# Where the gain and bias of the first feed-forward part's norm are applied to the residual rows

## The chip, the cores and the metric

The kernel runs on one core of a Trainium2 chip. The metric is the device time of one run in microseconds (us). The core has a matmul engine (TensorE, PE in the rows), a vector engine (VectorE, DVE), a scalar engine (ScalarE, ACT), a general engine (GpSimd, POOL) and a queue engine (SyncE, SP) that issues most transfers. Each engine works through its own list of instructions, and semaphores between the lists carry the dependences.

## The reference

The reference is a two-layer encoder trunk in float32 on 512 tokens of width 1024. Layer 0 mixes tokens by latent attention, layer 1 by a Hyena operator; a gated feed-forward part of width 2816 follows each. Behind every part stands the same residual norm:

```python
x <- layer_norm(DEEPNORM_ALPHA * x + f(x), g, b)      # (x - mean) * rsqrt(var + eps) * g + b

def hyena_mixer(x, ...):
    u = dwconv_centred(x @ w_in, w_short)             # 3 x 1024 features, a 3-tap convolution along the tokens
    v, g1, g2 = jnp.split(u, 3, axis=-1)
    z = v
    for o, gate in enumerate((g1, g2)):
        z_f = jnp.fft.rfft(z, n=2 * length, axis=1)
        y = jnp.fft.irfft(z_f * k_f, n=2 * length, axis=1)[:, :length]
        z = gate * (y + d_bias[o] * z)
    return z @ w_o

def conv_ffn(x, w_up, w_conv, w_down):
    a, g = jnp.split(dwconv_centred(x @ w_up, w_conv), 2, axis=-1)
    return (silu(g) * a) @ w_down
```

The norm's gain g and bias b therefore go two ways: into the next part's input, and into the residual row that the next norm adds.

## The kernel before

The four parts run in turn: attention, feed-forward part 0, Hyena, feed-forward part 1. Every projection is a float32 product in three passes of matmuls with split operands (lines 281 to 283: `xh,whi`, `xl,whi`, `xh,wlo`). The high halves come from ScalarE (line 274 for activations, 341 for weights), the low ones from VectorE (line 276, and 344 or 380 for weights). The tokens lie in four tiles t of 128.

**The tail of a part** (`tail`) projects back to the model width in two halves of 512 columns (names `dn`). `residual` adds the stored row, 1.414 times it, on VectorE (line 671) and takes statistics (line 674); `norm` makes mean and scale (lines 695, 696, 441, 443, 445, 449) and the normalised row (line 714); `put_x` transposes it on TensorE (line 287, name `xTps`) and applies gain and bias in the transposed form on ScalarE (line 541, name `xg`), since there they lie along the partitions. The same normalised row is also the residual of the next part: `save` stores it to DRAM with GpSimd's DMA (line 735, name `xsave`), and the next tail's `loads` fetches it again (line 629, name `xres`).

**Where the stored row gets its gain and bias** depends on the argument `late`. Without it, the tail loads the two vectors as rows over all partitions (`lngb`, line 629), and `save` multiplies and adds them on GpSimd, two steps for each half of 512 columns (line 733): 16 products for the four tiles. With `late`, the row is stored bare; the next tail then loads the two vectors ahead of its rows, and `apply` puts them on with VectorE (line 654), again 16 products, before `residual` may use a row. Attention's tail and the Hyena tail are `late`, the first feed-forward tail is not. The last tail, whose output leaves the chip, has no `save`.

**The Hyena part** projects 24 features (name `u`, each 8 x 3 matmuls) and puts a short convolution on each (line 1208 on ScalarE, 1210 and 1212 on VectorE). Features of the first two kinds are then transposed (line 287, name `utps`). Eight filter steps `long_conv` follow, two orders of four channel chunks: a forward transform on TensorE (line 1596, name `dft`), a chain of products on VectorE (line 1573, names `zt`, `zf`, `kf`; 20 of 512 elements a row and 4 of 1024), and an inverse transform on TensorE (line 1655 for order 0, 1673 for order 1, name `inv`) with one more product (`u<-inv`). A forward transform has two pairs of matmul groups; all but the first two products of the chain need the second pair. The results of order 1 are split and are the left side of the tail's `dn` matmuls, so the tail's matmuls begin while the last filter steps run. The output weights come in pieces, and SP loads them, the first weights of feed-forward part 1 and the tail's rows in one order.

**What sets the order.** The program is written as tasks that name, before each instruction, its engine and a rough cost. A list scheduler (class `Order`) resumes whichever task could start first by those costs, also with a limited count of blocks, accumulators and convolution slots, and each engine's queue gets the instructions in that order. Nothing else orders them: an edit to one task can alter the order of all engines from there on.

Of the kernel before, what the change touches and what calls it, by code (L numbers as in the profile page):

```python
# [21 lines left out]
P = 128  # L22
# [22 lines left out]
# The program is written as tasks (generators) that name, before each  # L45
# instruction, its engine and rough cost. A small list scheduler resumes them in
# the order in which a core would get to them; each engine's queue gets that order.
# [38 lines left out]
class Pending:  # L86
    """An event that waits for n parts."""
# [12 lines left out]
class Order:  # L100
# [25 lines left out]
    def step(self, task, value):  # L126
        """Resume a task and keep it where its next request is looked for."""
# [16 lines left out]
    def run(self):  # L144
        while True:
# [41 lines left out]
            if r[1] == "PE":  # L187
                # its clock is halved until it has been busy for a while
                if start - self.free.get("PE", -1e9) > COLD:
                    self.cold = COLD  # L190
                if self.cold > 0.0:
                    more = min(cost, self.cold / 2)
                    self.cold -= 2 * more
                    cost += more
# [39 lines left out]
class Trunk:  # L234
# [35 lines left out]
    def split(self, hi, lo, src, n, t, psum=False):  # L270
        """hi, lo: float32r parts of src, exact to the last bits."""
# [17 lines left out]
    def weights(self, src, shape, own=True, low=None, cut=False):  # L289
        """A task that loads a piece of a weight, 4 KB a partition, and splits it; its event.  # L290
        own: in the room for weights, else in two blocks. low: where its low part lies in DRAM, if it does.
        cut: in two transfers."""
# [59 lines left out]
    def low_part(self, src, shape, prio):  # L352
        """A task that puts the low part of a piece of a weight into DRAM ahead of its use; its event."""
# [38 lines left out]
    def columns(self, prio):  # L392
        """The vectors that lie along partitions, one column for each 128 values; their event."""
# [12 lines left out]
    def reduce_angle(self, r, ang, wide, t):  # L406
        """r = ang less the nearest multiple of 2 pi, within [-pi, pi]."""
# [27 lines left out]
    def rsqrt(self, y, m, t):  # L435
        """y = (-2 m) ** -0.5 for a few columns, with one Newton step."""
# [15 lines left out]
    def fm(self, ps, w, n, x, after, halves=False):  # L452
        """ps [P features, S] = sum over k of w(k)^T x(k), float32 in three passes.
        x(k): (hi, lo, event of the first half of the tokens, event of the second)."""
# [22 lines left out]
    def setup(self):  # L477
# [6 lines left out]
        # the array's clock is full only after a few us of work  # L484
# [8 lines left out]
    class X:  # L493
        """Feature-major x in float32r parts: two tiles of 128 features a block."""
# [23 lines left out]
    def put_x(self, x, t, src, times, gain=None):  # L518
        """Token tile t of x from token-major src [P, D]; times: when each half is there.
        gain: event of the columns, and where a gain and a bias to apply on the way lie in them."""  # L520
# [30 lines left out]
    def load_x(self):  # L551
        """The transposed x, laid out as [4, P, 2, S]."""
# [29 lines left out]
    def tail(self, base, lhs, w, nk, g, b, last, free_lhs, late, low=(), beats=()):  # L582
        """x <- LayerNorm(ALPHA x + lhs^T w), token-major; lhs(k): (hi, lo, event).
        late: x is kept without its gain and bias, for the next part to apply. Returns the new x."""
# [31 lines left out]
        def loads():  # L616
# [3 lines left out]
            # the table of the square root ahead of the norm  # L620
# [27 lines left out]
        def apply(t, tm, pg):  # L648
            # the gain and the bias of the norm before
# [12 lines left out]
        def residual(t, half, pss, tms):  # L662
            """pss: the accumulators of a half's columns, tms: when they are there."""
# [15 lines left out]
        def tail_cuts(t, half):  # L679
            # the columns of a half; the last ones in two pieces  # L680
# [1161 lines left out]
```

## Time and profile before

| | us |
| --- | --- |
| median of 3 runs | 1267.77 |
| lowest, highest | 1266.93, 1268.64 |
| span of the profiled execution, from its first instruction to its last | 1262.5 |
| TensorE, VectorE, ScalarE, GpSimd busy in it | 1238.5, 943.5, 568.1, 81.6 |

The profile is of one execution. Its own time is not listed apart from the span; the median of the runs is 5.3 us above the span, and that is taken as what lies around it. Times in the rows count from the start of the span. The first feed-forward part's last `dn` matmul starts at 634.41 us, the first projection of the Hyena part at 642.64, the last inverse transform at 858.29, and the first `up` matmul of feed-forward part 1 at 891.31. A matmul's duration in a timeline includes its way through the array and overlaps the next one; what it costs TensorE is the distance to the next start. The same holds for VectorE, where the next operation starts a little before the last one's end. Idle time in brackets is that of the engine before the row, with the instruction that ended it.

### The profile page before, as it was taken

The page shows a single profiled execution, that of the slowest core. Times are in us where ns is not written, and L with a number is a line of the kernel's source. Part 1 is how long each engine was busy: PE and PEld are TensorE (multiplying, and loading weights), DVE is VectorE, ACT ScalarE, POOL GpSimd, SP SyncE. Part 2 cuts the span into 40 slices and gives each one's busy share as a digit, 9 for nine tenths or more (in the row PEclk, how much of TensorE's full clock was granted, in tenths as well). Part 3 has the DMA queues.
Part 4 walks back from the last instruction along what each step waited for, and adds up shares of the span by engine and source line. Part 5 has one row for each costly group of instructions (what it writes and reads, how often), then busy time and mean ns, then how long its engine had stood idle before and what let it go on. Part 6 is the DMA issues. An engine that isn't in the chain of part 4 may idle for free.

```text
span 1262.5 us, 16644 instructions
## 1 busy us (share of the span) xinstructions
PE 1238.5 (98%) x6246; PEld 1051.7 (83%) x6246; DVE 943.5 (75%) x1614; ACT 568.1 (45%) x1086; POOL 81.6 (6%) x140
## 2 busy tenths in 40 slices
PE   8999999999999999999979999999999999999997
PEld 6788888988888888888868888887988888888886
DVE  7898987799997678657677999996566665553626
ACT  5566655644444456534553333232744444433220
POOL 0101000000000001100260000000000000000000
PEclk9999999999999999999989999999999999999999
DMA  5201125543344378999955655456433322323621
GB/s 207 60 28 47 57 70 214 184 136 120 120 143 136 97 261 290 299 350 303 317 194 169 200 170 167 141 190 222 145 100 96 90 98 100 100 89 113 233 67 67
DMA packets 67020, 195.47 MB, mean 155 GB/s; under 512 B 6873, under 2 KB 10713, under 8 KB 66940
## 3 DMA queue, kind: packets, MB, share of 16 engines
q1 hardware_dynamic: 53692, 146.17, 35.4%
q0 software_dynamic: 13248, 48.24, 11.0%
q8 instruction: 49, 0.80, 0.3%
q14 instruction: 31, 0.25, 0.1%
HBM read 160.83 MB, written 33.55 MB: 154 GB/s over the span
## 4 chain that ended last, share of the span: by engine, by line
PE 90%; DVE 4%; DMA 3%; ACT 2%; SPq 0%; issue 0%; DVEq 0%; ACTq 0%
PE up L282 12%; PE up L281 12%; PE up L283 12%; PE dn L281 7%; PE dn L283 7%; PE dn L282 7%; PE u L282 3%; PE u L283 3%; PE u L281 3%; PE dft L1596 2%; PE pTps L287 1%; PE inv L1673 1%; DMA wraw<-in_ffn_w_down_dram 1%; PE inv L1655 1%; ACT xg L541 1%; DVE xl L276 1%
## 5 line engine op out<-in xcount | busy, mean ns | idle before, releaser
L281 PE MATMUL up<-xh,whi 128*128 128x512 f32 (+1 forms) x768 | 286.1, 372 | 0.0
L282 PE MATMUL up<-xl,whi 128*128 128x512 f32 (+1 forms) x768 | 285.5, 372 | 0.0
L283 PE MATMUL up<-xh,wlo 128*128 128x512 f32 (+1 forms) x768 | 285.2, 371 | 0.0
L341 ACT CAST whi<-wraw 128x512 fp32r<-128x512 f32 (+1 forms) x376 | 216.3, 615 | 121.7 <-PE dn L283 94.0
L344 DVE TENSOR_TENSOR wlo<-wraw,whi 128x512 fp32r<-128x512 f32 (+1 forms) x312 | 207.3, 678 | 80.4 <-ACT whi L341 80.1
L283 PEld LDWEIGHTS up<-xh,wlo 128*128 128x128 f32 x768 | 144.6, 188 | 25.1
L281 PEld LDWEIGHTS up<-xh,whi 128*128 128x128 f32 x768 | 144.7, 188 | 24.5
L282 PEld LDWEIGHTS up<-xl,whi 128*128 128x128 f32 x768 | 144.7, 188 | 24.3
L1210 DVE SCALAR_TENSOR_TENSOR cv<-up,cols,cv 128x511 f32<-128x511 f32 x88 | 65.6, 748 | 112.7 <-ACT cv L1208 112.7
L281 PE MATMUL dn<-whi,gated 128*128 128x512 f32 (+1 forms) x374 | 141.4, 378 | 0.1
L282 PE MATMUL dn<-wlo,gated 128*128 128x512 f32 (+1 forms) x374 | 140.9, 377 | 0.0
L283 PE MATMUL dn<-whi,gated 128*128 128x512 f32 (+1 forms) x374 | 140.9, 377 | 0.0
L1208 ACT ACTIVATE cv<-up,cols 128x512 f32<-128x512 f32 x88 | 60.4, 689 | 166.7 <-PE up L283 166.5
L281 PE MATMUL u<-xh,whi 128*128 128x512 f32 (+1 forms) x224 | 87.1, 389 | 0.0
L282 PE MATMUL u<-xl,whi 128*128 128x512 f32 (+1 forms) x224 | 81.5, 364 | 1.6 <-DVE xl L276 1.6
L281 PEld LDWEIGHTS dn<-whi,gated 128*128 128x128 f32 x374 | 70.4, 188 | 13.3 <-DVE xres L671 0.5
L283 PE MATMUL u<-xh,wlo 128*128 128x512 f32 (+1 forms) x224 | 81.3, 363 | 0.0
L283 PEld LDWEIGHTS dn<-whi,gated 128*128 128x128 f32 x374 | 70.4, 188 | 13.0
L282 PEld LDWEIGHTS dn<-wlo,gated 128*128 128x128 f32 x374 | 70.4, 188 | 12.7
L1212 DVE SCALAR_TENSOR_TENSOR cv<-up,cols,cv 128x511 f32<-128x511 f32 x88 | 65.2, 743 | 0.0
L1573 DVE TENSOR_TENSOR zf<-zt 128x512 f32<-128x512 f32 x80 | 51.5, 682 | 0.0
L541 ACT ACTIVATE xg<-xTps,cols 128x128 f32<-128x128 f32 x96 | 38.3, 466 | 27.2 <-PE xTps L287 27.2
(244 smaller groups left out, 2149.7 us busy)
## 6 DMA issues: line engine op xcount, KB each, us to landing
wraw<-in_ffn_up_dram SPq DMA_DIRECT2D x91, 512.0 KB, 3.6
wraw<-in_hy_in_dram SPq DMA_DIRECT2D x46, 512.0 KB, 6.8
wraw<-in_ffn_w_down_dram SPq DMA_DIRECT2D x44, 512.0 KB, 4.5
low<-wlo POOLq DMA_DIRECT2D x32, 512.0 KB, 7.2
wlo<-low POOLq DMA_DIRECT2D x32, 512.0 KB, 3.7
kf<-kfs POOLq DMA_DIRECT2D x16, 512.0 KB, 3.1
kf<-kf SPq DMA_DIRECT2D x16, 512.0 KB, 7.0
wraw<-in_hy_w_o_dram SPq DMA_DIRECT2D x15, 512.0 KB, 6.5
```

Of the source, the lines that this page charges most:

```text
L276: nc.vector.tensor_tensor(lo, src, hi.bitcast(F32), op=ALU.subtract)
L281: mm(ps, lh, rh, start=first, stop=False)
L282: mm(ps, lh, rl, start=False, stop=False)
L283: mm(ps, ll, rh, start=False, stop=last)
L341: nc.scalar.copy(hi[:, s], raw[:, s])
L344: nc.vector.tensor_tensor(lo[:, s], raw[:, s], hi[:, s].bitcast(F32), op=ALU.subtract)
L541: nc.scalar.activation(v[:, j, :], ps[:, j, :], AF.Identity, scale=gb[:, at + d:at + d + 1], bias=gb[:, at + ND + d:at + ND + d + 1])
L1208: nc.scalar.activation(dst, ps, AF.Copy, scale=taps(1))
L1210: nc.vector.scalar_tensor_tensor(dst[:, 1:], ps[:, :S - 1], taps(0), dst[:, 1:], op0=ALU.mult, op1=ALU.add)
L1212: nc.vector.scalar_tensor_tensor(dst[:, :S - 1], ps[:, 1:], taps(2), dst[:, :S - 1], op0=ALU.mult, op1=ALU.add)
L1573: tt = lambda d, a, b, f: nc.vector.tensor_tensor(d, a, b, op=f)
L1596: nc.tensor.matmul(q[:, w], tab[:, r, w], z[:, r], start=True, stop=True)
```

## The change

The first feed-forward tail becomes `late`, as attention's tail and the Hyena tail are. Its row loads of gain and bias and its 16 GpSimd products go, and its four stores hold bare normalised rows. The Hyena tail now loads gain and bias (two more transfers of 512 KB, ahead of its four rows, in two more blocks) and applies them with 16 VectorE products of 128 x 512 (line 654) ahead of line 671. The rest of the diff drops comments. Its core, in `ffn`:

```diff
@@ -1275,10 +1275,10 @@
         return self.tail(base + 2.0, lambda k: (gated[k] and gated[k][:, 0, :], gated[k] and gated[k][:, 1, :], gev[k]),
-                         a["ffn_w_down"][i], NF, a["ln2_g"][i], a["ln2_b"][i], last, free_lhs, False,
+                         a["ffn_w_down"][i], NF, a["ln2_g"][i], a["ln2_b"][i], last, free_lhs, not last,
                          beats=self.beats[2 * NF:] if i == 0 else [])
```

Since the tasks' steps and the blocks they hold differ, the scheduler writes the queues anew from the end of feed-forward part 0 to the end of the Hyena tail; from feed-forward part 1 on the order is the same. Three places show it.

**VectorE in the middle of the Hyena part.** A feature is projected (`u_6908`, `u_6956`), goes through the short convolution (`u_7143`, `u_7215`) and is transposed by TensorE (`utps_7289` before, `utps_7344` now). Before, the convolution's two steps stand here, the second of them 33 instructions on (counted with both) from the first product of the forward transform `dft_7100` (`zt_7006<-dft_7100`):

```order
L1573 TENSOR_TENSOR zt_7171<-dft_7182,e2_7186 128x512
L1573 TENSOR_TENSOR zt_7006<-zf_7004,kf_7002 128x1024
L1573 TENSOR_TENSOR zt_7171<-dft_7182,e2_7186 128x512
L1573 TENSOR_TENSOR kf_7002<-zf_7004,kf_7002 128x1024
L1210 SCALAR_TENSOR_TENSOR u_7143<-u_6908,cols_101,u_7143 128x511
L1573 TENSOR_TENSOR zf_7004<-kf_7002 128x512
L1212 SCALAR_TENSOR_TENSOR u_7143<-u_6908,cols_101,u_7143 128x511
L1573 TENSOR_TENSOR zf_7004<-zt_7006 128x512
L1573 TENSOR_TENSOR zt_7172<-dft_7278,e2_7282 128x512
```

In the changed queue, the second step of the counterpart stands 45 instructions on (counted with both) from the first product of `dft_7162` (`zt_7024<-dft_7162`), and another feature's steps (`u2_6963`) stand ahead of it:

```order
L1573 TENSOR_TENSOR zt_7111<-dft_7200,e2_7207 128x512
L1573 TENSOR_TENSOR zf_7021<-zt_7023,zt_7024 128x512
L1210 SCALAR_TENSOR_TENSOR u2_6963<-u_7002,cols_101,u2_6963 128x511
L1573 TENSOR_TENSOR zf_7021<-zt_7023,zt_7024 128x512
L1212 SCALAR_TENSOR_TENSOR u2_6963<-u_7002,cols_101,u2_6963 128x511
L1573 TENSOR_TENSOR zf_7022<-zt_7023,zt_7024 128x512
L1210 SCALAR_TENSOR_TENSOR u_7215<-u_6956,cols_101,u_7215 128x511
L1573 TENSOR_TENSOR zf_7022<-zt_7023,zt_7024 128x2x256
L1573 TENSOR_TENSOR zt_7112<-dft_7324,e2_7331 128x512
L1212 SCALAR_TENSOR_TENSOR u_7215<-u_6956,cols_101,u_7215 128x511
L1573 TENSOR_TENSOR zt_7112<-dft_7324,e2_7331 128x2x256
```

The convolution moved behind the whole chains of two filter steps. In the trace before, TensorE ends `dft_7100` at 728.76 and starts `utps_7289` at 753.91; now, between `dft_7162` and `utps_7344` lie 78 projection matmuls and two transforms.

**VectorE at the last filter step** (order 1, last chunk). Before, its products are mixed with the end of the step ahead (`u_7572`, its `xl`) and with short convolutions (`u_7694`), and TensorE has matmuls of several kinds between the last `dft` and the first of the last two `inv` groups:

```order
L1573 TENSOR_TENSOR zt<-zf,kf 128x1024
L1573 TENSOR_TENSOR u_7572<-inv,u_7572 128x4x128
L1573 TENSOR_TENSOR kf<-zf,kf 128x1024
L276 TENSOR_TENSOR xl<-u_7572,xh 128x512
L1573 TENSOR_TENSOR zf<-kf 128x512
L1212 SCALAR_TENSOR_TENSOR u_7694<-u,cols,u_7694 128x511
L1573 TENSOR_TENSOR zf<-zt 128x512
L1573 TENSOR_TENSOR u_7572<-inv,u_7572 128x4x128
L1573 TENSOR_TENSOR zt<-zf 128x512
L1210 SCALAR_TENSOR_TENSOR u_7694<-u,cols,u_7694 128x511
L276 TENSOR_TENSOR xl<-u_7572,xh 128x512
L1573 TENSOR_TENSOR zt<-zf 128x512
```

In the changed queue, the step's products stand by themselves, from its first to the end:

```order
L1212 SCALAR_TENSOR_TENSOR u_7662<-u,cols,u_7662 128x511
L1573 TENSOR_TENSOR zt<-dft,e_7977 128x512 x2
L1573 TENSOR_TENSOR zt<-dft,e_8006 128x512
L1573 TENSOR_TENSOR zt<-dft,e_8006 128x2x256
L1573 TENSOR_TENSOR zf<-zt 128x2x256 x3
L1573 TENSOR_TENSOR zf<-zt 128x512
L1573 TENSOR_TENSOR zt<-zf,kf 128x1024
L1573 TENSOR_TENSOR kf<-zf,kf 128x1024
L1573 TENSOR_TENSOR zf<-kf 128x512
L1573 TENSOR_TENSOR zf<-zt 128x512
L1573 TENSOR_TENSOR zt<-zf 128x512 x2
L1573 TENSOR_TENSOR zt<-zf,kf 128x1024
```

What was mixed in moved ahead of the chain, and on TensorE 18 `dn` matmuls now stand between the last `dft` and both last `inv` groups.

**VectorE in the Hyena tail**, from the last inverse products (`u<-inv`) to the first residual of token tile 0. Before:

```order
L1573 TENSOR_TENSOR u_7694<-inv,u_7694 128x4x128
L276 TENSOR_TENSOR xl<-u_7694,xh 128x512
L1573 TENSOR_TENSOR u_7694<-inv,u_7694 128x4x128
L276 TENSOR_TENSOR xl<-u_7694,xh 128x512
L344 TENSOR_TENSOR wlo<-wraw,whi 128x512 x2
L671 SCALAR_TENSOR_TENSOR xres<-xres,dn_7828 128x512
L344 TENSOR_TENSOR wlo<-wraw,whi 128x512 x2
L674 BN_STATS st<-xres 128x6
```

And in the changed queue:

```order
L1573 TENSOR_TENSOR u_7662<-inv,u_7662 128x4x128
L276 TENSOR_TENSOR xl<-u_7662,xh 128x512
L1573 TENSOR_TENSOR u_7662<-inv,u_7662 128x4x128
L276 TENSOR_TENSOR xl<-u_7662,xh 128x512
L654 TENSOR_TENSOR xres<-xres,lngb 128x512 x11
L344 TENSOR_TENSOR wlo<-wraw,whi 128x512 x2
L654 TENSOR_TENSOR xres<-xres,lngb 128x512 x4
L671 SCALAR_TENSOR_TENSOR xres<-xres,dn_7781 128x512
L654 TENSOR_TENSOR xres<-xres,lngb 128x512
L674 BN_STATS st<-xres 128x6
```

Fifteen of the 16 added products stand ahead of the first residual, eleven of them ahead of the low part of a weight piece (line 344). On SP the two row loads stand between the second weight load for feed-forward part 1 and the four `xres` loads.

## Rows read from the trace of the kernel before

**Rows 1.** The page: the busy line of the engines, the shares of the chain that ended last by engine, and of the costliest groups the gain and bias columns that ScalarE applies behind the transposes (busy us, mean ns of one, idle before).

```profile
PE 1238.5 (98%) x6246; PEld 1051.7 (83%) x6246; DVE 943.5 (75%) x1614; ACT 568.1 (45%) x1086; POOL 81.6 (6%) x140
...
PE 90%; DVE 4%; DMA 3%; ACT 2%; SPq 0%; issue 0%; DVEq 0%; ACTq 0%
...
L541 ACT ACTIVATE xg<-xTps,cols 128x128 f32<-128x128 f32 x96 | 38.3, 466 | 27.2 <-PE xTps L287 27.2
```

**Rows 2.** Busy time in stretches of 25 us: stretch, its length, busy us (and instructions) of PE, PEld, DVE, ACT and POOL, granted TensorE clock, DMA share, GB/s. The first stretch holds the end of the first feed-forward part and the start of the Hyena part, the second lies in the middle of the Hyena part, the third at its end.

```profile
625.00:650.00 25.00, 17.90 (x102) 15.75 (x101) 21.80 (x33) 15.37 (x43) 16.76 (x16) 0.86 0.58 196
...
725.00:750.00 25.00, 25.00 (x115) 21.10 (x114) 24.43 (x37) 7.79 (x14) 2.15 (x4) 1.00 0.50 157
...
850.00:875.00 25.00, 23.82 (x120) 19.67 (x119) 16.61 (x26) 6.85 (x13) 1.61 (x3) 1.00 0.71 259
```

**Rows 3.** Timeline of TensorE from the end of the first feed-forward part into the Hyena projections: start, duration, engine, line, operation, tiles, count, and in brackets the idle time before it with what ended it. Between the first two rows shown lie 17 more projection matmuls of 256 columns.

```profile
641.91 1.08 PE L287 MATMUL xTps<-ident,xres 128*128 128x128 f32 x4 [7.10 <-DVE xres L714]
...
646.26 0.28 PE L283 MATMUL u<-xh,wlo 128*128 128x256 f32 x1
646.38 0.28 PE L281 MATMUL u<-xh,whi 128*128 128x256 f32 x1
...
652.29 0.28 PE L281 MATMUL u<-xh,whi 128*128 128x256 f32 x1
653.13 0.39 PE L282 MATMUL u<-xl,whi 128*128 128x256 f32 x1 [0.56 <-DVE xl L276]
653.35 0.28 PE L283 MATMUL u<-xh,wlo 128*128 128x256 f32 x1
...
655.97 0.38 PE L282 MATMUL u<-xl,whi 128*128 128x256 f32 x1 [1.07 <-DVE xl L276]
```

**Rows 4.** Timeline of VectorE at the same place, same columns.

```profile
625.08 0.22 DVE L445 SCALAR_TENSOR_TENSOR nt<-rs,mv 128x1 f32<-128x1 f32 x1
...
627.56 0.95 DVE L276 TENSOR_TENSOR xl<-xg,xh 128x256 fp32r<-128x256 f32 x2
...
631.35 4.18 DVE L276 TENSOR_TENSOR xl<-xg,xh 128x256 fp32r<-128x256 f32 x3 [1.04 <-ACT xh L274]
...
635.65 3.29 DVE L445 SCALAR_TENSOR_TENSOR nt<-rs,mv 128x1 f32<-128x1 f32 x1
...
639.05 1.99 DVE L276 TENSOR_TENSOR xl<-xg,xh 128x256 fp32r<-128x256 f32 x1
```

**Rows 5.** The view of line 733, all 16 of its GpSimd products together: min/median/max ns, first and last start.

```profile
L733 POOL TENSOR_TENSOR xres<-xres,lngb x16: 1272/1296/1476, 628.5 to 656.2; 128x512 f32<-128x512 f32 x16
```

**Rows 6.** Timeline of VectorE in the middle of the Hyena part: products of two filter chains (line 1573) and the end of one short convolution (line 1212). The pitch of an operation is its start to the next start.

```profile
729.85 0.68 DVE L1573 TENSOR_TENSOR zt<-dft,e 128x512 f32<-128x512 f32 x1
...
741.68 1.22 DVE L1573 TENSOR_TENSOR kf<-zf,kf 128x1024 f32<-128x1024 f32 x1
742.82 0.68 DVE L1573 TENSOR_TENSOR zf<-zt 128x512 f32<-128x512 f32 x1
743.42 0.68 DVE L1573 TENSOR_TENSOR zf<-kf 128x512 f32<-128x512 f32 x1
...
752.36 0.74 DVE L1212 SCALAR_TENSOR_TENSOR u<-u,cols 128x511 f32<-128x511 f32 x1
753.02 0.68 DVE L1573 TENSOR_TENSOR zf<-zt 128x512 f32<-128x512 f32 x1
```

**Rows 7.** Timeline of TensorE there: a forward transform, and the next transposes of a projected feature.

```profile
727.03 1.89 PE L1596 MATMUL dft<-u,dft 128*128 128x256 f32 x8
...
753.91 0.63 PE L287 MATMUL utps<-ident,u 128*128 128x128 f32 x4
```

**Rows 8.** The chain of waits towards the end of the Hyena part: start, duration from start to start, what.

```profile
820.32 0.23 PE u L281
...
827.51 1.73 PE dft L1596 x8
...
855.29 1.78 PE inv L1673 x16
```

**Rows 9.** Timeline of TensorE at the last inverse transforms (line 1673) and the last wait of the Hyena part.

```profile
855.13 1.95 PE L1673 MATMUL inv<-dft,zf 128*128 128x128 f32 x16
...
862.11 0.50 PE L281 MATMUL dn<-whi,xh 128*128 128x512 f32 x1 [1.18 <-ACT xh L274]
```

**Rows 10.** Timeline of VectorE from the last filter chain into the Hyena tail.

```profile
838.07 1.07 DVE L1573 TENSOR_TENSOR u<-inv,u 128x512 f32<-128x512 f32 x1
...
852.22 2.49 DVE L1573 TENSOR_TENSOR zf<-zt 128x512 f32<-128x512 f32 x4
...
867.74 0.68 DVE L671 SCALAR_TENSOR_TENSOR xres<-xres,dn 128x512 f32<-128x512 f32 x1
...
876.58 0.81 DVE L714 TENSOR_SCALAR xres<-xres,mv,rs 128x1024 f32<-128x1024 f32 x1
```

**Rows 11.** Timeline of the SP queue (DMA issues) at the Hyena tail.

```profile
852.46 7.82 SPq L312 DMA_DIRECT2D wraw<-in_ffn_up_dram  x2
860.38 1.93 SPq L629 DMA_DIRECT2D xres<-xsave  x4
```

**Rows 12.** Timeline of VectorE in the tail of the second feed-forward part, where line 654 applies rows already.

```profile
1179.46 4.29 DVE L654 TENSOR_TENSOR xres<-xres,lngb 128x512 f32<-128x512 f32 x7
```

**Rows 13.** The view of line 629, the loads of the tails: who waited for them (us, times), the line on VectorE.

```profile
  DVE xres L654: 6.1, 3
```

## The prediction

> **What bounds the kernel now.** I read three views in turn. The page's busy line and chain [rows 1] show TensorE busy 98% of the 1262.5 us span and holding 90% of the chain that ended last: an edit is worth what it adds to or takes from TensorE's idle time. VectorE's or GpSimd's own time counts only where TensorE waits for it. The busy times by 25 us [rows 2] show where TensorE has idle time around the change: 7.1 us at 625 to 650, at a granted clock of 0.86, and 1.18 us at 850 to 875. In the middle of the Hyena part (725 to 750) it is busy all 25.00 us, with VectorE at 24.43. The two engines are level there, and TensorE is full only because the two queues are ordered so that each result is there in time. The change has the scheduler write those queues anew. So the third view is the timeline where one queue hands over to the other [rows 3, 4, 6 to 10], laid beside the order of the changed queues. Every duration below is read from the trace before; only counts and positions come from the new order. The sum is made on the span and carried to the median, 1267.8 us; the 5.3 us that lie around the span are kept.
>
> **A. The GpSimd products leave the first feed-forward norm: a gain of 5.5 us (3 to 10).** TensorE stands 7.10 us in front of transposes until VectorE's normalised rows come [rows 3]. VectorE is late there because of single steps: 3.29 us for a one-column step that takes 0.22 elsewhere, 4.18 us for three and 1.99 us for one 256-element subtraction, where two took 0.95 [rows 4]. All of them run while GpSimd is in its 16 products, 1.3 us each [rows 5]. Above the usual this is 3.1 + 2.8 + 1.5 = 7.4 us, the whole wait. [...] Two more waits follow, 0.56 and 1.07. Ceiling: 7.10 + 2 + 0.56 + 1.07 = 10.7 us.
>
> Not all of it returns. In the new order all the last token tile's down matmuls run in one piece and only three projection matmuls stand ahead of the third tile's transposes, so TensorE arrives early and waits: by the usual durations of its steps VectorE is some 8 us from the end of that tile's down matmuls to its normalised rows (an estimate), against 6.4 of TensorE work, which leaves 1.3 to 2.5 us of wait. ScalarE's gain and bias steps, 0.47 us each and four to a transpose group [rows 1], keep 1 to 4 us of waits in front of the first projections. I take 5 left, a gain of 5.5.
>
> [...]
>
> **B. The new order in the middle of the Hyena part: a loss of 10.1 us.** The PE queue now holds 78 projection matmuls and two forward transforms between the transform dft_7162 and the transposes utps_7344: 78 x 0.23 + 2 x 1.73 = 21.4 us [rows 8]. Those transposes need u_7215, whose last step stands in VectorE's queue 45 instructions on from the first product of dft_7162: eight of 1024 elements, four short-convolution steps, 33 others. By the pitches 1.14, 0.66 and 0.60 [rows 6] that is 9.1 + 2.6 + 19.8 = 31.5 us. None of the 45 can start before that transform, so TensorE must stand for 31.5 - 21.4 = 10.1 us. The same count on the kernel before gives 23.1 us, and its trace has 729.85 to 753.10, or 23.25 [rows 6]; TensorE reaches the transposes 25.2 us after the transform's end, at 753.91, without a wait [rows 7]. There VectorE's chain just fits; in the new order it doesn't.
>
> **C. The last filter chain: a loss of 10.1 + 0.5 us.** Before, TensorE had 25.9 us of projections, inverse transforms and down matmuls between the end of the last forward transform, 829.24 [rows 8], and the inverse at 855.13, which it reached without a wait [rows 9]. Now 18 down matmuls follow, 4.1 us, and then the inverse. From the transform VectorE needs 16 products of 512 and four of 1024 elements until the first half can be inverted: 9.6 + 4.6 = 14.2 us at the pitches of rows 6 (four took 2.49 in this chain before [rows 10]). Wait: 14.2 - 4.1 = 10.1 us. Both inverses now stand together with nothing between, so the wait behind them, 1.18 before [rows 9], grows by some 0.5.
>
> **D. The clock: a loss of 4 us (0 to 4).** [...]
>
> **E. The Hyena tail: a loss of 4 us (2 to 10).** Sixteen products of 0.61 us (4.29 for seven [rows 12]), 9.8 us, enter VectorE's queue between the last subtraction and the first residual, with the two casts for the last weight piece behind eleven of them. Down matmuls cover most: from the last inverse to the first transposes TensorE has 20.5 us of work and some 2 of waits, VectorE 3 + 10.2 (the products and casts) + 10.5 to the first normalised row (before 867.74 to 877.39, 9.7 [rows 10]), so 1.2 to 1.8 us are left over. The second tile's last transposes now stand 0.5 us ahead of the second feed-forward part, whose matmuls then wait about 1.6 us for ScalarE. The two added loads go through SP ahead of the four rows, which left at 860.38 behind two weight loads [rows 11]. In the new order they can leave during the wait of C. Bounds: nothing, or the 6.1 us that VectorE waits for the loads where a tail does this already [rows 13]; I take 1. Cover gone, E is some 10.
>
> **Sum.** 1267.8 - 5.5 + 10.1 + 10.6 + 4 + 4 = **1291.0 us**. The ends: B and C together are 20.2 at the pitches, with no time between the engines, and 25.5 at the full durations in place of the pitches (0.68, 1.22, 0.74 [rows 6]); the 23.1 against 23.25 above speaks for the pitches. With 0 to 4 for D, 2 to 7 for E (its late loads are a rival) and 10 to 3 of gain for A, the forecast's own range is 1280 to 1302.
>
> **The rivals.** *Faster:* neither queue holds TensorE up, because it runs free matmuls past the waiting transposes and inverse. For it speaks that projections and down matmuls with their data ready do stand behind both. Then A and E remain, at best -10 + 2: 1260 us. It decides at utps_7344: if TensorE starts a later projection before it, this rival holds. Against it: at 652.29 a pass was done, its second waited until 653.13 for the subtraction, and the third, whose operands were there, came at 653.35 [rows 3]. [...] 7%. *No change:* the order costs nothing for the same reason and A is eaten by E: 1267.8 - 5.5 + 4 = 1266.3 us; 4%. *One wait only:* one of B and C is filled, 1291.0 - 10.1 - 2 = 1279 us; 5%. *Later than forecast:* the loads of E leave only after the down matmuls, as at 860.38 before, and A gives 3: 1291 + 6 + 2.5 = 1299.5 us; 6%.
>
> **How the numbers follow.** The forecast case has 78%. A measurement of this kernel tells about 0.2% from no change (its three times spread 1.7 us). Faster by more than that: 7%; within it: 4%; slower: 78 + 5 + 6 = 89%. The range of 1278 to 1302 takes in the forecast's own, the one-wait case and the late loads; left out are the two cases near or below 1267 and the outer ends of the rest, under 2 in 10.
>
> **What would show it.** In the profile after, A: no GpSimd products, no VectorE step of 3 us for one column, the idle time in front of the third tile's transposes under 3 us. B: one idle of 9 to 11 us in front of utps transposes, released by VectorE's line 1212, about 120 us into the Hyena part, with VectorE busy all through it. C: an idle of like size in front of an inverse of line 1673, released by line 1573. D: lower granted clock in both stretches. E: waits of 1 to 2 us in front of the first transposes and the first up matmul. The forecast is wrong if the Hyena part from the first projection to the last inverse takes about as long as before: then VectorE's pitch in these chains is far below 0.60, or TensorE found other work.

## The result, and the profile after

The changed kernel takes 1283.12 us (median of 4 runs, 1281.03 to 1285.13); the kernel before, run beside it, 1268.01 (4 runs, 1266.93 to 1268.64). The ratio is 1.0127, with a 95% interval of 1.011 to 1.0144: 14 to 18 us slower.

The profiled execution of the changed kernel took 1284.07 us with a span of 1282.3, so 1.8 us lie around the span. The 5.3 us that the prediction kept there for the kernel before were for the most part the distance of its one profiled execution from the median (an execution with that span, 1262.5, took 1264.28). The span grew by 19.8 us, the median by 15.1; a sum over the two traces has to come to the first. Of the 19.8, 2.2 us are not the change's: TensorE's order is the same in both kernels up to the 3140th matmul, at the end of feed-forward part 0, and that one starts at 623.70 in the trace after and at 621.55 in the trace before; part 0's first `up` matmul, long before any difference between the kernels, is late by 2.7 already (221.85 against 219.17). In the ten profiled executions of this document it starts anywhere from 621.00 to 628.32, so two traces are best compared from there on.

The busy line of the page after:

```profile
PE 1247.1 (97%) x6246; PEld 1055.7 (82%) x6246; DVE 940.8 (73%) x1630; ACT 567.5 (44%) x1086; POOL 61.0 (5%) x124
```

Beside [rows 1], GpSimd has 16 instructions fewer and VectorE 16 more, and yet VectorE is busy 2.7 us less: the steps that used to be stretched beside GpSimd cost less than before. (Experiment 4 below is the kernel before without these products; its VectorE is busy 930.6 us against 943.5.) The same 6246 matmuls hold TensorE 8.6 us longer; the rest of the growth is idle time.

Where it went shows in the busy times by 25 us of the kernel after (stretch, length, PE, PEld, DVE, ACT, POOL, granted clock, DMA share, GB/s):

```profile
625.00:650.00 25.00, 24.96 (x169) 22.84 (x169) 17.25 (x43) 21.05 (x58) 5.28 (x9) 1.00 0.97 330
...
725.00:750.00 25.00, 25.00 (x115) 21.04 (x114) 20.89 (x30) 6.27 (x11) 1.07 (x2) 1.00 0.47 147
750.00:775.00 25.00, 16.81 (x61) 12.81 (x60) 23.91 (x37) 4.99 (x9) 1.07 (x2) 0.73 0.38 126
...
850.00:875.00 25.00, 14.32 (x64) 12.12 (x64) 18.49 (x26) 4.06 (x8) 1.61 (x3) 0.81 0.74 260
```

At the norm TensorE is busy 24.96 of 25 us, where it was 17.90 [rows 2]: the moved work paid. In the middle of the Hyena part 16.81 us are left, with VectorE at 23.91, and at its end 14.32, where it was 23.82 [rows 2]. In both stretches the granted clock fell, to 0.73 and 0.81.

**At the norm.** TensorE after, at the second tile's last transposes (636.55), at the third tile's first (638.07), which are the ones that it waited for before, and at the only wait that is marked among the first projections (answers to [rows 3]):

```profile
636.55 0.60 PE L287 MATMUL xTps<-ident,xres 128*128 128x128 f32 x4
...
638.07 0.60 PE L287 MATMUL xTps<-ident,xres 128*128 128x128 f32 x4
...
653.33 0.38 PE L281 MATMUL u<-xh,whi 128*128 128x256 f32 x1 [0.91 <-ACT xh L274]
```

The 7.10 us of waiting in front of the third tile's transposes are gone. VectorE writes that tile's normalised row just ahead of them:

```profile
636.67 0.81 DVE L714 TENSOR_SCALAR xres<-xres,mv,rs 128x1024 f32<-128x1024 f32 x1
```

Line 445, the one-column step of the norm, over the whole kernel after (minimum, median and maximum in ns):

```profile
L445 DVE SCALAR_TENSOR_TENSOR nt<-rs,mv x16: 219/219/223, 208.0 to 1275.9; 128x1 f32<-128x1 f32 x16
```

None of the 16 is stretched; before, one took 3.29 us [rows 4].

**In the middle of the Hyena part.** TensorE after, from the forward transform that the prediction calls dft_7162 to the transposes utps_7344 (answers to [rows 7]):

```profile
732.10 1.89 PE L1596 MATMUL dft<-u,dft 128*128 128x256 f32 x8
...
754.64 1.13 PE L1596 MATMUL dft<-u,dft 128*128 128x256 f32 x4 [2.36 <-ACT e L1602]
760.17 0.79 PE L281 MATMUL u<-xh,whi 128*128 128x512 f32 x1 [4.40 <-DVE zt L1573]
760.76 0.63 PE L282 MATMUL u<-xl,whi 128*128 128x512 f32 x1
...
765.80 1.13 PE L287 MATMUL utps<-ident,u 128*128 128x128 f32 x4 [1.43 <-DVE u L1212]
```

From the transform's end, 732.10 + 1.73 = 733.83, to the transposes are 32.0 us for 21.4 us of work. The loss is one of three waits, 2.36 + 4.40 + 1.43 = 8.2 us, and of matmuls that step by 0.43 after them where 0.23 is usual (granted clock 0.50 from 760.20 to 764.20 and from 765.80 to 769.70, 1.00 from there to 775). A listed duration lies above the step by 0.16 us at 256 columns and at 512: 0.28 and 0.12 [rows 3], 0.39 and 0.23 (769.95). VectorE's queue in between, its first and its last step (answers to [rows 6]):

```profile
734.10 0.69 DVE L1573 TENSOR_TENSOR zt<-dft,e 128x512 f32<-128x512 f32 x1
...
764.99 0.76 DVE L1212 SCALAR_TENSOR_TENSOR u<-u,cols 128x511 f32<-128x511 f32 x1
```

From 734.10 to 765.75 are 31.65 us. The transposes could start as soon as this was through, and did.

**At the end of the Hyena part.** TensorE after, from the last forward transform to the first transposes of the tail (answers to [rows 9]):

```profile
855.87 1.89 PE L1596 MATMUL dft<-u,dft 128*128 128x256 f32 x8
...
872.54 5.26 PE L1673 MATMUL inv<-dft,zf 128*128 128x128 f32 x32 [10.68 <-DVE zf L1573]
...
880.25 0.50 PE L281 MATMUL dn<-whi,xh 128*128 128x512 f32 x1 [1.18 <-ACT xh L274]
...
900.82 0.66 PE L287 MATMUL xTps<-ident,xres 128*128 128x128 f32 x4 [0.28 <-DVE xres L714]
```

One idle of 10.68 us in front of the last inverse transforms, released by line 1573 on VectorE; before, TensorE reached that place without a wait [rows 9]. The SP queue meanwhile (answers to [rows 11]):

```profile
855.92 7.52 SPq L312 DMA_DIRECT2D wraw<-in_ffn_up_dram  x2
863.49 0.42 SPq L629 DMA_DIRECT2D lngb<-in_ln_g_dram  x1
863.97 0.60 SPq L629 DMA_DIRECT2D lngb<-in_ln_b_dram  x1
864.66 2.03 SPq L629 DMA_DIRECT2D xres<-xsave  x4
```

The added loads leave during that idle, and the added products, on VectorE, run under the down matmuls:

```profile
880.84 6.71 DVE L654 TENSOR_TENSOR xres<-xres,lngb 128x512 f32<-128x512 f32 x11
888.66 2.50 DVE L654 TENSOR_TENSOR xres<-xres,lngb 128x512 f32<-128x512 f32 x4
891.07 0.69 DVE L671 SCALAR_TENSOR_TENSOR xres<-xres,dn 128x512 f32<-128x512 f32 x1
```

The 0.28 us in front of the first transposes are all that these leave of themselves there.

Three places that both kernels have, in us from the span's start:

| | before | after | after - before |
| --- | --- | --- | --- |
| first Hyena projection | 642.64 | 636.20 | -6.4 |
| first `up` matmul of feed-forward part 1 | 891.31 | 909.92 | +18.6 |
| end of the last matmul | 1254.27 | 1274.08 | +19.8 |

All but the last 1.2 us of the loss is there by the end of the Hyena tail, and of the Hyena part and its tail the change gives new work to the tail alone.

### The profile page after: what moved, and what is told of

It reads as the page before. It is cut to its first block, busy times and chain, and to the rows that moved or that the text cites. A ratio compares the mean times of both kernels' runs of the same rounds, so it can differ in the third digit from the quotient of the medians.

```text
span 1282.3 us, 16645 instructions
## 1 busy us (share of the span) xinstructions
PE 1247.1 (97%) x6246; PEld 1055.7 (82%) x6246; DVE 940.8 (73%) x1630; ACT 567.5 (44%) x1086; POOL 61.0 (5%) x124
## 4 chain that ended last, share of the span: by engine, by line
PE 88%; DVE 6%; ACT 3%; DMA 2%; issue 1%; SPq 0%; DVEq 0%; ACTq 0%
PE up L282 12%; PE up L283 12%; PE up L281 12%; PE dn L283 8%; PE dn L282 8%; PE dn L281 8%; PE u L282 3%; PE u L281 3%; PE u L283 3%; PE dft L1596 2%; DVE zt L1573 1%; ACT xg L541 1%; DVE zf L1573 1%; PE pTps L287 1%; PE inv L1673 1%; PE inv L1655 1%
## 5 line engine op out<-in xcount | busy, mean ns | idle before, releaser
L281 PEld LDWEIGHTS u<-xh,whi 128*128 128x128 f32 x224 | 43.3, 193 | 12.3 <-DVE zt L1573 4.8
```

What stands on the lines that cost most here:

```text
L281: mm(ps, lh, rh, start=first, stop=False)
```

## The experiments

The theory is the prediction's: what is lost is the price of the new order of the queues, which the scheduler writes once the costs and blocks of the moved steps are booked elsewhere; the moved work by itself is a gain at the norm and a small cost in the tail. The rival: the moved work costs what is lost (loads and products in the tail, or VectorE too full), and the order is neutral. So the experiments part order and work. An instruction can be booked with the scheduler (`op(...)`, `get(...)`) without being issued, and issued without being booked; that holds the order still while the work is changed, and the other way round. Each ratio is to the kernel before, run beside it (medians of 1266.45 to 1266.53 us).

**1. The edit in the order of before** (e1_edit_in_old_order). The changed kernel; the scheduler still books the two blocks and the GpSimd products at the norm. Against the changed kernel:

```
+        ghost = 2 if late and len(beats) else 0
...
-            tb = yield get("blk", 4 + len(rows) + len(xgain))
+            tb = yield get("blk", 4 + len(rows) + len(xgain) + ghost)
...
+            for _ in range(2 * ghost):
+                tm = yield op("POOL", pool2(512), tm, tg)
```

> The change, but the scheduler is made to believe that the first feed-forward tail still holds two more blocks and still does its products, so that all five queues keep the order of the kernel before up to the Hyena tail. Theory (the loss is the new order of the Hyena part, the moved products themselves are a gain at the norm): no idle of TensorE over 2 us in the Hyena part, 9 us gained at the norm, 3 to 7 us lost in the Hyena tail, since the two added loads now leave at about 860 us; 1262 to 1266 us, ratio 0.995 to 0.998. Rival (the loss is the work that was added to the Hyena tail: 16 VectorE products and two loads): about as slow as the changed kernel, 1278 to 1285 us.

Measured: 1269.44 us (10 runs), ratio 1.0019 (1.0004 to 1.0034). Neither had it. The idles of the Hyena part are gone (750 to 775: TensorE busy 25.00 us at a clock of 1.00), as the theory wants. But the tail's work, which costs next to nothing in the changed kernel, is here a wait of 12 us. VectorE, TensorE and SP at the tail of this kernel:

```profile
862.83 9.24 DVE L660 TENSOR_TENSOR xres<-xres,lngb 128x512 f32<-128x512 f32 x15 [1.45 <-DMA xres<-xsave]
```

```profile
881.11 1.12 PE L287 MATMUL xTps<-ident,xres 128*128 128x128 f32 x4 [12.23 <-DVE xres L720]
```

```profile
844.38 7.82 SPq L312 DMA_DIRECT2D wraw<-in_ffn_up_dram  x2
852.30 0.38 SPq L630 DMA_DIRECT2D lngb<-in_ln_g_dram  x1
...
853.25 2.72 SPq L630 DMA_DIRECT2D xres<-xsave  x4
```

Two weight loads hold SP, the rows leave only at 853.25, VectorE cannot begin the products before 862.83, and TensorE has run out of down matmuls at 868.9. The theory's size for the tail was wrong in this order: uncovered, the moved work makes a wait of 12 us, with slower matmuls behind it (the `dn` matmuls from 882.45 on step by 0.43, those up to 868.49 by 0.23). From the last inverse transforms (850.21) to the first `up` matmul (898.50) are 48.3 us, where the kernel before takes 33.0 (858.29 to 891.31). That is more than the move gains at the norm.

**2. The old work in the new order** (e2_old_work_in_new_order). The queues of the changed kernel, with the GpSimd products issued at the norm and no products or loads in the tail. The products take the row's other half as second operand, so gain and bias are left out.

```
+                    if q is not None:
+                        nc.vector.tensor_tensor(xres[t][:, hs], xres[t][:, hs], q[:, hs], op=f)
...
+            for h in range(2 if own else 0):
...
+                    nc.gpsimd.tensor_tensor(z[:, hs], z[:, hs], z[:, os], op=f)
```

> The queues in the order of the changed kernel, but with the work of the kernel before: 16 GpSimd products at the first feed-forward norm (their second operand is the other half of the row instead of gain and bias, which are not loaded) and no products in the Hyena tail. Theory: the two idle stretches of TensorE in the Hyena part are there, 20 us and some 4 of clock, and the gain at the norm is not: 1286 to 1293 us. Rival (added work in the tail): that work is gone, so 1265 to 1270 us.

Measured: 1292.12 us (4 runs), ratio 1.0196 (1.0173 to 1.022), within the theory's range. The kernel that does the old work in the new order is the slowest of all; the rival falls. Its windows show both troubles at once, the norm's and the order's:

```profile
625.00:650.00 25.00, 20.98 (x116) 18.37 (x114) 22.54 (x36) 15.39 (x42) 17.50 (x17) 0.93 0.71 239
...
750.00:775.00 25.00, 17.14 (x64) 12.93 (x63) 25.00 (x37) 4.19 (x8) 1.08 (x2) 0.77 0.51 178
```

**3. The new order without the products** (e3_new_order_no_products), as experiment 2, but nothing is issued on GpSimd either; gain and bias are left out of the residual.

```
-            for h in range(2 if own else 0):
+            for h in range(0):
```

> The queues in the order of the changed kernel, without any products: neither the GpSimd ones at the first feed-forward norm nor the VectorE ones and their two loads in the Hyena tail (gain and bias are left out of that residual). Against the changed kernel it shows what the products and loads in the tail cost by themselves. Theory: 0 to 3 us less than the changed kernel, 1279 to 1284 us, with both idle stretches as there. Rival: the tail's work is the loss, so 1257 to 1262 us.

Measured: 1281.49 us (4 runs), ratio 1.0112 (1.0088 to 1.0137). Within the theory's range. The changed kernel, which does all of the tail's work, takes 1283.12, but the kernel before took 1268.01 beside it and 1266.45 here: loads and products together are worth between 0.1 us (growth against growth) and 1.6 (time against time), which these runs don't tell apart. The idle in front of the last inverse transforms is 10.68 us here and in experiment 2, as in the changed kernel, so the added loads have no part in it.

**4. The old order without the products** (e4_old_order_no_products), as experiment 1, with nothing loaded or multiplied in the tail; the same part is left out.

```
-        self.xgain = [g, b] if late else []
+        self.xgain = [g, b] if late and not ghost else []
```

> The kernel before in its own order, all queues alike, without the 16 GpSimd products and their two loads (gain and bias are left out of the residual that the Hyena tail adds). It shows what the products beside the norm cost by themselves. Theory: the 7.1 us idle before the transposes, the clock behind it and the two small waits go, 8 to 10 us: 1258 to 1260 us, ratio about 0.993. Rival (VectorE's late rows have another cause, and the GpSimd products are hidden): 1266 to 1268 us.

Measured: 1254.87 us (5 runs), ratio 0.9906 (0.988 to 0.9933). A gain of 11.6 us (8.5 to 15.2), more than expected. TensorE passes from the last down matmuls to the transposes without a wait. Experiments 1 to 4 and the two kernels make a table of two orders and three kinds of work (us):

| | products on GpSimd at the norm | none | on VectorE in the tail |
| --- | --- | --- | --- |
| order of before | 1266.5 | 1254.9 | 1269.4 |
| order of the change | 1292.1 | 1281.5 | 1283.1 |

The 1283.1 is the one time measured beside another sample of the kernel before (1268.0). Down a column, the new order costs 25.6 and 26.6 us where the tail is free of products, and 13.7 where they are in the tail, since there the old order pays for them and the new one covers them. Along a row, the products at the norm cost 11.6 and 10.6.

**5. Products on VectorE, but at the norm** (e5_products_on_vector_at_norm). The kernel before, its 16 products put on VectorE behind the last tile's transposes; all the work is done.

```
+            if rows:
+                tl, _ = yield wait(xnew.put[NT - 1])
+                tm = max(tm, tl)
...
-                    tm = yield op("POOL", pool2(512), tm, tg)
-                    nc.gpsimd.tensor_tensor(z[:, hs], z[:, hs], q[:, hs], op=f)
+                    tm = yield op("DVE", dve(512), tm, tg)
+                    nc.vector.tensor_tensor(z[:, hs], z[:, hs], q[:, hs], op=f)
```

> The kernel before, with its 16 products next to the first feed-forward norm on VectorE instead of GpSimd, behind the last tile's transposes, ahead of the first short convolutions; the stored row keeps gain and bias, the Hyena tail is as before. The scheduler writes the Hyena queues anew here too. Theory (gain at the norm of about 11 us, but a new order of the Hyena part with TensorE in wait for VectorE's chains): one idle stretch of 8 to 9 us in pieces in the middle of the Hyena part, with 3 to 4 us of clock, none at the last filter step; 1264 to 1270 us. Rival (where the products run is all that counts): 1255 to 1259 us.

Measured: 1268.74 us (10 runs), ratio 1.0019 (1.0004 to 1.0034), as the theory expected. It has no wait at the norm and none at the last filter step. Here too the scheduler wrote new queues, and TensorE shows waits of the same kind in the middle of the Hyena part (window 750 to 775: 17.02 us busy, clock 0.80), with the same releasers:

```profile
757.05 0.80 PE L281 MATMUL u<-xh,whi 128*128 128x512 f32 x1 [4.95 <-DVE zt L1576]
...
762.74 0.82 PE L287 MATMUL utps<-ident,u 128*128 128x128 f32 x4 [2.06 <-DVE u L1215]
```

**6. The edit in the old order, with earlier loads** (e6_old_order_early_loads). Experiment 1 showed what the tail lacks: rows that are there in time. The loads are asked for one weight piece earlier; all the work is done. Against experiment 1:

```
-                    if c == (nk2 - GO if nk2 > 4 else nk2 - 1) and half == 0:
+                    if c == (nk2 - GO if nk2 > 4 else nk2 - 1 if not xgain else 2) and half == 0:
```

> As e1 (the change in the old order), but the Hyena tail's loads of gain, bias and rows are asked for one chunk of the output projection earlier (with chunk 2 of half 0 in place of chunk 3), so that they stand ahead of two weight loads on SP, and its 16 products fall between the last filter products on VectorE. Theory (the 12.4 us wait of e1 is the late landing of the rows plus 15 products in one piece ahead of the first residual): the wait falls below 2 us and the gain at the norm is kept: 1255 to 1260 us, ratio 0.991 to 0.995, faster than the kernel before and the changed one. Rival (16 products more on VectorE cost about their 9.8 us wherever they stand in the tail): 1264 to 1268 us.

Measured: 1261.34 us (5 runs), ratio 0.9961 (0.9948 to 0.9974): faster than both kernels, though short of what was expected. SP, VectorE and TensorE at its tail:

```profile
841.11 3.14 SPq L630 DMA_DIRECT2D xres<-xsave  x4
```

```profile
850.44 0.69 DVE L660 TENSOR_TENSOR xres<-xres,lngb 128x512 f32<-128x512 f32 x1 [3.05 <-DMA xres<-xsave]
```

```profile
854.32 0.50 PE L283 MATMUL dn<-whi,xl 128*128 128x512 f32 x1 [0.70 <-DVE xl L276]
...
856.59 0.50 PE L281 MATMUL dn<-whi,xh 128*128 128x512 f32 x1 [1.77 <-ACT xh L274]
...
875.98 0.60 PE L287 MATMUL xTps<-ident,xres 128*128 128x128 f32 x4
```

The rows leave 12 us earlier than in experiment 1, and the transposes have no wait. In its place stand some 3 us of small waits at down matmuls, whose left sides VectorE splits between the products, and behind them matmuls that step by 0.43, up to 861.62.

**7. Nothing changed but a cost** (e7_old_work_other_cost). The kernel before with all its instructions; the scheduler is told that a GpSimd product, the 16 at the norm, takes less:

```
 def pool2(n):
-    return 90 + 2.1 * n
+    return 90 + 1.4 * n
```

> The kernel before with all of its instructions, 16 GpSimd products included; only the scheduler's rough cost of such a product is a third lower (90 + 1.4 n in place of 90 + 2.1 n nanoseconds for n columns), which alters the order of the queues from there to the Hyena tail. Theory (the time hangs on the order of the Hyena queues, which any small difference ahead of them alters): idle stretches of TensorE of 8 to 9 us in the middle of the Hyena part and 3 to 4 us of clock: 1275 to 1282 us. Rival (the order of equal work costs nothing): 1265 to 1269 us.

Measured: 1279.97 us (4 runs), ratio 1.0112 (1.0089 to 1.0135). The same instructions as before, none moved to another engine, and 13.4 us slower, with the waits of the changed kernel at the same three kinds of place. TensorE in the middle of the Hyena part of this kernel:

```profile
760.98 1.13 PE L1596 MATMUL dft<-u,dft 128*128 128x256 f32 x4 [1.68 <-ACT e L1602]
767.07 0.80 PE L281 MATMUL u<-xh,whi 128*128 128x512 f32 x1 [4.95 <-DVE zt L1573]
...
772.76 0.75 PE L287 MATMUL utps<-ident,u 128*128 128x128 f32 x4 [1.99 <-DVE u L1212]
```

The last inverse transforms have no wait here, so this is the loss of the middle alone. An order by itself makes it.

**8. The changed kernel with shorter chains** (e8_new_order_short_chains). Its queues are kept, without the 32 VectorE products of 1024 elements, so that the multiplication by the filter is left out:

```
             t = yield op("DVE", dve(1024), t, tk)
-            tt(tmp[i], x[i], kf[i][:, ::-1], ALU.mult)
             t = yield op("DVE", dve(1024), t)
-            tt(kf[i], x[i], kf[i], ALU.mult)
```

> The changed kernel with its queues in the same order, but without the 32 filter products of 1024 elements on VectorE (the multiplication by the filter is left out). Theory (TensorE waits for VectorE's chains): the eight of them that lie in the middle chain, 9.1 us, and the four in the last one, 4.6 us, come off the two waits: under 3 us left in the middle, about 6 at the last inverse, and less lost to the clock; 1265 to 1270 us. Rival (TensorE waits there for loads, or for room that the scheduler holds back): the waits stay, 1280 to 1285 us.

Measured: 1266.52 us (10 runs), ratio 1.0004 (0.9995 to 1.0014), as expected of VectorE's chains being what TensorE waits for. The waits shrink as the chains do. TensorE of this kernel:

```profile
751.77 0.50 PE L281 MATMUL u<-xh,whi 128*128 128x512 f32 x1 [1.49 <-ACT e L1602]
...
853.67 6.14 PE L1671 MATMUL inv<-dft,zf 128*128 128x128 f32 x32 [5.52 <-DVE zf L1573]
```

The last idle falls from 10.68 to 5.52 us, by 5.2; the four products of 1024 elements that stood ahead of it take 5.0 us in the changed kernel's trace (861.60 to 864.12 and 866.66 to 869.17).

## Why the prediction was right, and where its sizes were off

The direction and the mechanism were right, and the time lies inside the range, 7.9 us under the forecast. Two terms were mis-sized, A and E, both so that the loss came out too large, by 3.8 and 2.3 us. The rest is in the base: the sum was worked out from a trace and laid on the median. The forecast loss is 23.2 us, the terms as measured come to 17.4 in the traces, and from median to median the kernel lost 15.1.

- **A, the norm: forecast -5.5, measured -9.3.** Idle time and slower matmuls took 11.5 us there before and take 2.2 after. Experiments 4 against before and 3 against 2 give 11.6 and 10.6. The mis-sized term is the 5 us that were to be left over. The first part of it was a wrong reading of the queue: the transposes behind three projection matmuls, to which the 6.4 us of TensorE work were counted, are the second tile's last (636.55). The third tile's stand behind these and nine more projection matmuls, at 638.07, 8.2 us from the end of that tile's down matmuls (629.84). VectorE has the row ready at 637.48, 7.6 us from there, near the 8 that were estimated; so TensorE does not come early, and the wait of 1.3 to 2.5 is nothing. For the second part, ScalarE's gain and bias steps leave one wait of 0.91, the low end of 1 to 4. The ceiling of 10.7 was the better value. Its 2 us are slower matmuls, 1.95 us by the trace before: four transposes and 17 projection matmuls take 0.73 and 3.62 us there (641.91 to 646.26, granted clock 0.52), and 0.36 (653.47 to 653.83) and 17 x 0.12 at a granted clock of 1.00. That the stretched steps come from GpSimd's products is shown by line 445 above, and by experiment 3 against 2, which differ at the norm in these products alone (experiment 4 leaves out their two loads as well).
- **B, the middle of the Hyena part: forecast +10.1, measured +10.6.** VectorE's chain was forecast at 31.5 us and took 31.65, TensorE has the 21.4 us of work that were counted. Only the place was partly wrong: one idle was forecast in front of utps_7344, and three pieces came. TensorE was held up already at the forward transforms in between and at the projections behind them, by ScalarE's and VectorE's readings of the transforms' results (`e`, `zt`); only 1.43 us were left for the transposes. The sum doesn't change, since the same chain of VectorE decides when they may start.
- **C, the last filter chain: forecast +10.1 and 0.5, measured +10.7.** The wait is 10.68 us, released by line 1573, as forecast; the 0.6 above it is for the most part the pitch of the four products of 1024 elements, 1.26 in this chain where 1.14 was taken. The 0.5 behind the inverses didn't come: 1.18 us before [rows 9] and after. Experiment 8 shows the chain as the cause.
- **D, the clock: forecast +4, measured 3.7.** No run shows the 4 us of the sum, its lower end of 0, or the 2 in the rival *one wait only*: they were the author's estimate. What the runs show in their place are slower matmuls behind the waits: some 2.0 us after the transposes of B, until 769.7, where the matmuls of projections step by 0.43 in place of 0.23 (granted clock 0.50); and 1.7 us in the two inverses, 5.26 against 2 x 1.78 [rows 8] (granted clock 0.72 from 872.54 to 877.80). What slower matmuls cost inside B's stretch stands in B. B's wait came in three pieces, with a granted clock of 0.73 in 750 to 775.
- **E, the tail: forecast +4 (2 to 10), measured 1.7.** TensorE loses 0.28 us in front of the first transposes (1.2 to 1.8 were forecast) and, among the first `up` matmuls, 0.38 and 0.64 us above their usual step at 913.32 and 920.03 (1.6 were forecast; 0.38 of the second is a wait for VectorE's line 276); the other 0.4 us is not located. The two at the `up` matmuls are the order's and not the moved work's: experiment 3 has neither products nor loads in the tail, and the same two steps, at 911.62 and 918.32. What the moved work leaves is 0.6 us: from the third `dn` matmul behind the inverses to the first `up` matmul are 31.3 us after (878.58 to 909.92), and 30.8 both before (860.54 to 891.31) and in experiment 3 (877.45 to 908.22). The loads left during C's wait, as taken: 863.49 is 9 us ahead of the last inverses (872.54). In experiment 1, without that wait, the first of them leaves at 852.30, behind the start of the last inverse (850.21), and the wait alone is 12.23 us, above the 10 that the prediction gave as E's upper end. So E is small because C covers it, and the range for it held only with that cover.

Measured together: -9.3 + 10.6 + 10.7 + 3.7 + 1.7 = 17.4 us, of 19.8. Another 2.2 stand ahead of the change's first effect (623.70 against 621.55, above), and 0.2 us are not assigned.

Of the rivals, *faster* was to be decided at utps_7344, by whether TensorE starts a later projection before it. It doesn't: TensorE stands idle for 1.43 us in front of them, and the next projection matmul starts behind them, at 766.59, with no wait of its own. Nor does any trace of this order show a matmul taken ahead: the 6246 matmuls start in one and the same order in the changed kernel and in experiments 2, 3 and 8, whose waits differ (in front of the last inverse transforms 10.68 us in the first three and 5.52 in experiment 8). *No change* and *one wait only* fall with B and C, which both came in full; *later than forecast* falls with the loads at 863.49.

The cause of the loss is settled as far as these runs go: the order makes it (experiments 2 and 3, and 7 for the middle of the Hyena part), through VectorE's chains (experiment 8). The moved work does not: without it the loss stays (experiment 3), and with all of it in the old order, once the rows come in time, the kernel is faster than before (experiment 6). Two things stay open. Experiment 6 does all the work and lies 6.5 us above experiment 4, which does none of the products. The traces show 3.8 us of it in the tail: from the last inverse transforms to the first `up` matmul are 36.8 us in experiment 6 (850.97 to 887.72) and 33.0 in experiment 4 (854.70 to 887.68). The rest isn't located. And it wasn't tried whether the changed kernel, with the order repaired in the Hyena part alone, comes below experiment 6.

## What to carry to other kernels

Where a planner writes the queues, every edit is two: the work that it moves, and the order that it causes elsewhere. Count the second on the changed queues, engine against engine (work on the one between two points, chain on the other between the same points), and part the two on the chip by booking a step without issuing it. A step that is free under another engine's wait is no longer free once that wait is repaired: experiment 1 took away the 18.9 us of waits in the Hyena part and gave back 12.2 in the tail, until the loads were moved as well.

## What was not expected of the hardware

A VectorE step with one tensor operand was stretched beside GpSimd, too. VectorE in experiment 2, the step that writes the second tile's normalised row, with GpSimd's products running from 629.59 on, and the same step in experiment 3, which has the same order and no such products:

```profile
629.30 2.16 DVE L725 TENSOR_SCALAR xres<-xres,mv,rs 128x1024 f32<-128x1024 f32 x1
```

```profile
626.86 0.81 DVE L725 TENSOR_SCALAR xres<-xres,mv,rs 128x1024 f32<-128x1024 f32 x1
```

The same step takes 2.16 us and 0.81 us. So in these runs not only the two-operand steps [rows 4] were stretched beside the products. Not every overlap shows it: the next such step of experiment 2 starts at 641.62, a product starts beside it at 641.97, and the step takes 0.81. And TensorE's waits spread: a chain that ends at one pair of transposes held TensorE up at two places ahead of them as well (2.36 and 4.40 us), since forward transforms that stand in between need their results read by the same busy engines.
